# A two-layer hybrid decoder trunk on one core: the second layer's instructions placed by an event loop in place of the framework's scheduler

## Chip, core and metric

The kernel runs on one core of one Trainium2 chip, as one program. The metric is the device time in microseconds (us) from the program's start to its end; a kernel's time is the median of its runs. The engines are named as in the profile: PE (TensorE, matmul), PEld (its weight loads), DVE (VectorE), ACT (ScalarE), POOL (GpSimd) and SP (SyncE, which here issues nearly all DMAs). Each engine works off a queue of its own in the order in which the instructions stand there, and waits at an instruction until what it needs is done.

## What is computed

Two residual layers over 2048 tokens of width 1024 (float32). Layer 1 mixes by gated linear attention, layer 2 by dilated window attention in three groups of six heads; both add attention into 256 memory tokens, a SiLU gate and an output projection. The change lies in layer 2 and at the seam to it.

```python
DIL_GROUPS = ((128, 1), (512, 4), (2048, 16))   # window, dilation
DIL_HEADS, DIL_HEAD_DIM = 6, 128

def dilated_group(q, k, v, window, dilation):
    # tokens are sorted by phase (position mod dilation) and cut into blocks of 128;
    # each block sees itself and the block before it
    s = jnp.einsum('bphjqd,bphjkd->bphjqk', qb, kw) * (Dh ** -0.5)
    s = jnp.where(mask, s, -jnp.inf)
    m = jnp.max(s, axis=-1, keepdims=True)
    p = jnp.exp(s - m)
    den = jnp.sum(p, axis=-1, keepdims=True)
    o = jnp.einsum('bphjqk,bphjkd->bphjqd', p / den, vw)
    return o, (m + jnp.log(den))[..., 0]

def dilated_mixer(h, w_in):
    for g, (window, dil) in enumerate(DIL_GROUPS):
        qkv = (h @ w_in[:, base:base + 3 * 768]).reshape(B, T, 3, 6, 128)
        q, k = partial_rope(qkv[:, :, 0], pos), partial_rope(qkv[:, :, 1], pos)
        o, lse = dilated_group(q, k, qkv[:, :, 2], window, dil)
    wts = jax.nn.softmax(jnp.stack(lses, axis=0), axis=0)     # over the groups
    o = jnp.einsum('gbth,gbthd->bthd', wts, jnp.stack(outs, axis=0))
    q_mem, gate = jnp.split(h @ w_in[:, 3 * 3 * 768:], [256], axis=-1)
    return o, q_mem, gate

def reference(x, mem, ...):
    for i in range(2):
        h = rmsnorm(x, norm_w[i])
        mix, q_mem, gate = (gla_mixer if i == 0 else dilated_mixer)(h, ...)
        mem_o = memory_attention(q_mem, mem_n, w_memkv[i])
        x = x + (jnp.concatenate([mix, mem_o], -1) * jax.nn.silu(gate)) @ w_out[i]
    return rmsnorm(x, final_norm_w)
```

## The kernel before

**What sets the order.** The kernel is written against a tile framework. Pools hand out buffers, the framework adds the waits, and a scheduler inside it places each engine's instructions by a timeline of its own; the order in which the code emits them is a starting point. Nothing in layer 1 or 2 is fixed by hand before the change.

**Layer 1** ends with a stage that takes the 16 token blocks in pairs: `a2_q`, `a2_gate`, `a2_branch`, `a2_out`, `a2_norm`, and `a2_pair`, which forms seven sums and differences of the normalised rows (the left operands of a Strassen-Winograd scheme: seven products of half-size blocks in place of eight). Each is split into a high and a low fp16 part, transposed by DMA and kept as a tile `h2s[half][0..6]`, some straight in SBUF and some through DRAM (`h2_d`).

**Weight sets.** Layer 2's input projection is cut into 28 sets of 256 columns: nine for values (`v`), eighteen for queries and keys (`qk`, one head each) and one for the memory queries (`m`); four more sets are the gate. `load_ws` (L847) loads a set in float32 (`stg`), for `qk` scales one half of it (L853), and makes the seven right operands `w`: ACT writes the high part (L859), DVE the low part (L860), POOL the differences between (L863 to L869).

**Products.** `sw_half` (L875) runs one set against one half of the rows: seven products, each of 48 matmuls of 128 columns (values) or 12 of 512 columns (queries, keys, gates). Each goes to a PSUM bank from `mm_bank` (L832), which takes turns among five banks (`ps_mm` twice over, `ps_x`, `ps_tr`). ACT copies three results out (`snap`, L896: p1, u2, u3), POOL adds p1 to two of these, DVE adds a bank to a copy (`addto`, L901, tile `cx`), and `fin` splits each finished block into high and low (`hl`, L965 on ACT, L966 on DVE) and stores it to DRAM. A rotary embedding follows for each half of a `qk` set (`xr`, `sw`, L1008 to L1023).

**Attention.** 18 heads of 8 steps make 144 steps. `att_load` brings q, k and v back from DRAM. `att_scores` (L1054) computes two blocks of scores into `ps_g`, DVE takes the masked row maximum (L1087, `mx`, result `pm`) and the bias `st` (L1091), ACT the exponential (L1097). `split_P` makes high and low parts `ph` (ACT L168, POOL L169) and transposes them by DMA to `pt` (L170). The value products (`pv`, L1112) then read `pt` into `ps_o`. After eight steps `att_stats` transposes the statistics `st` (L1142) and stores them. When three groups of a head pair are done, `combos` (L1184) mixes them; its loads (`fo`, `fb`) and its work on POOL and DVE are strewn in twice during the products and once at the gates.

**Interleaving.** The code emits products and attention by a fixed pattern: `advance(to)` emits products up to a count, each attention step follows its count (L1281 to L1302), values lag scores by a step and two products.

**Gates.** `gate_half` (L1225) computes a sigmoid (tile `e`): a clamp on POOL or, where the source is a PSUM bank, on DVE (L1233), three ACT functions (L1234 to L1236), a product with the mixed heads on POOL (L1237) and one with the gate input on DVE (L1238). Between the gate products stand 16 blocks of memory attention (`mem_stage`, L1330), whose weights `mp` pass through `split_P` as `mh`. The output projection (L1389 to L1437) takes 16 row blocks in turn.

## Time and profile before

| | |
|---|---|
| median of 3 runs | 2891.72 us (2888.61 to 2911.24) |
| profiled execution | 2893.61 us, span 2891.5 us |
| granted PE clock, mean | 0.950 |
| HBM traffic | 280.44 MB read, 136.76 MB written |
| hand-over of the layers | about 973 to 1009 us |
| products and attention of layer 2 | about 1009 to 2427 us |
| gates and memory attention | about 2427 to 2707 us |
| output projection | about 2707 us to the end |

The page's second part gives the span in 40 equal slices, with the busy share of each engine in tenths (9 is 90% or more), the clock granted to PE in tenths, and the share of the DMA engines:

```profile
PE   7999889899999399899998787999787898768799
PEclk9999989999999799999999999999999999878999
DMA  6234952456466735777666889675788776776533
```

A slice is 72.3 us. The fourteenth (a 3) is the hand-over between the layers. The 7s and 8s after it come in two groups, in which the mixes of the first and second head pairs run, and at the end in the gate stage.

### The profile page before, as it was taken

The page shows a single profiled execution, that of the slowest core. Times are in us where ns is not written, and L with a number is a line of the kernel's source. Part 1 is how long each engine was busy: PE and PEld are TensorE (multiplying, and loading weights), DVE is VectorE, ACT ScalarE, POOL GpSimd, SP SyncE. Part 2 cuts the span into 40 slices and gives each one's busy share as a digit, 9 for nine tenths or more (in the row PEclk, how much of TensorE's full clock was granted, in tenths as well). Part 3 has the DMA queues.
Part 4 walks back from the last instruction along what each step waited for, and adds up shares of the span by engine and source line. Part 5 has one row for each costly group of instructions (what it writes and reads, how often), then busy time and mean ns, then how long its engine had stood idle before and what let it go on. Part 6 is the DMA issues. An engine that isn't in the chain of part 4 may idle for free. (4 is left out here: it accounts for less than half of the span.)

```text
span 2891.5 us, 55208 instructions
## 1 busy us (share of the span) xinstructions
PE 2526.5 (87%) x21384; PEld 1897.8 (66%) x21384; DVE 1621.2 (56%) x3141; ACT 1326.7 (46%) x2969; POOL 967.1 (33%) x789
## 2 busy tenths in 40 slices
PE   7999889899999399899998787999787898768799
PEld 6888779788887374757574655766464765334587
DVE  6446544565556346565656566565557556654433
ACT  6356643553444244455444344444444445454422
POOL 0000000021112135444544556343455444776300
PEclk9999989999999799999999999999999999878999
DMA  6234952456466735777666889675788776776533
GB/s 204 82 131 161 293 168 86 125 134 154 107 149 155 210 115 152 187 170 174 157 167 175 206 212 194 163 184 146 201 203 203 179 165 167 185 185 170 193 132 123
DMA packets 807659, 481.81 MB, mean 167 GB/s; under 512 B 509234, under 2 KB 746468, under 8 KB 806244
## 3 DMA queue, kind: packets, MB, share of 16 engines
q1 hardware_dynamic: 807396, 478.28, 63.7%
q8 instruction: 168, 2.75, 0.4%
q14 instruction: 95, 0.78, 0.1%
HBM read 280.44 MB, written 136.76 MB: 144 GB/s over the span
## 5 line engine op out<-in xcount | busy, mean ns | idle before, releaser
L175 PE MATMUL ps_mm<-w,hT 128*128 128x256 f16 (+1 forms) x1408 | 390.8, 278 | 17.8 <-ACT v L529 6.2
L176 PE MATMUL ps_mm<-w,hT 128*128 128x256 f16 (+1 forms) x1408 | 390.0, 278 | 0.0
L177 PE MATMUL ps_mm<-w,hT 128*128 128x256 f16 (+1 forms) x1408 | 388.6, 278 | 0.4 <-DVE hT L421 0.4
L176 PEld LDWEIGHTS <-w 128*128 128x128 f16 x2032 | 210.2, 103 | 160.2 <-issue 46.7
L177 PEld LDWEIGHTS <-w 128*128 128x128 f16 x2032 | 209.7, 103 | 145.3 <-issue 14.5
L175 PEld LDWEIGHTS <-w 128*128 128x128 f16 x2032 | 210.4, 104 | 129.0 <-issue 12.3
L860 DVE SCALAR_TENSOR_TENSOR w<-stg,wsc,w 128x512 f16<-128x512 f32 x217 | 199.6, 920 | 160.6 <-ACT w L859 159.7
L169 POOL TENSOR_TENSOR stg<-mp,stg 128x512 f16<-128x512 f32 x16 | 18.9, 1180 | 724.4 <-ACT stg L168 724.4
L859 ACT ACTIVATE w<-stg,wsc 128x512 f16<-128x512 f32 x217 | 155.2, 716 | 201.7 <-DMA stg<-in_w_in_b 85.1
L1097 ACT ACTIVATE pm<-pm,st,qsc 128x256 f32<-128x256 f32 (+1 forms) x288 | 156.7, 545 | 180.0 <-DVE st L1091 179.2
L169 POOL TENSOR_TENSOR ph<-pm,ph 128x512 f16<-128x512 f32 (+2 forms) x144 | 149.6, 1040 | 210.4 <-ACT ph L168 122.6
L175 PE MATMUL ps_mm<-w,w 128*128 128x128 f16 (+1 forms) x744 | 186.4, 280 | 8.9 <-DVE cx L901 8.7
L966 DVE SCALAR_TENSOR_TENSOR hl<-cx,hl 128x512 f16<-128x512 f32 x162 | 140.1, 865 | 94.5 <-ACT hl L965 93.1
L176 PE MATMUL ps_mm<-w,w 128*128 128x128 f16 (+1 forms) x744 | 186.3, 280 | 0.0
L177 PE MATMUL ps_mm<-w,w 128*128 128x128 f16 (+1 forms) x744 | 186.0, 279 | 0.0
L965 ACT ACTIVATE hl<-cx 128x512 f16<-128x512 f32 x162 | 100.9, 623 | 184.9 <-DVE cx L901 158.7
L176 PEld LDWEIGHTS <-hT 128*128 128x128 f16 x1408 | 140.3, 100 | 39.6 <-issue 19.8
L175 PE MATMUL ps_o<-pt,v 128*128 128x128 f16 (+1 forms) x384 | 79.2, 235 | 86.9 <-DMA pt<-ph 86.8
L175 PEld LDWEIGHTS <-hT 128*128 128x128 f16 x1408 | 140.7, 100 | 21.2 <-issue 1.3
L177 PEld LDWEIGHTS <-hT 128*128 128x128 f16 x1408 | 140.5, 100 | 19.5 <-DVE hT L421 0.7
L918 POOL TENSOR_TENSOR u<-u,p 128x512 f32<-128x512 f32 x64 | 88.2, 1379 | 120.9 <-ACT u L896 119.9
L175 PEld LDWEIGHTS <-h 128*128 128x128 f16 x800 | 89.2, 112 | 37.7 <-issue 35.9
(419 smaller groups left out, 8087.7 us busy)
## 6 DMA issues: line engine op xcount, KB each, us to landing
stg<-in_w_in_b SPq DMA_DIRECT2D x144, 256.0 KB
stg<-in_w_in_b SPq DMA_DIRECT2D x54, 512.0 KB
qkd<-hl SPq DMA_DIRECT2D x144, 192.0 KB
rope<-in_rope SPq DMA_DIRECT2D x36, 512.0 KB
vud<-hl SPq DMA_DIRECT2D x72, 256.0 KB
q<-qkd SPq DMA_DIRECT2D x72, 256.0 KB
od<-osb SPq DMA_DIRECT2D x72, 256.0 KB
fb<-fd SPq DMA_DIRECT2D x72, 256.0 KB
```

The source lines that it names most:

```text
L169: G.tensor_tensor(out=lo, in0=src, in1=hi, op=ALU.subtract)
L175: PE.matmul(o, sh, mh, start=first, stop=False, skip_group_check=free)
L176: PE.matmul(o, sh, ml, start=False, stop=False, skip_group_check=free)
L177: PE.matmul(o, sl, mh, start=False, stop=last, skip_group_check=free)
L859: A.activation(out=t[:, 0], in_=src, func=AF.Copy, scale=s1)
L860: V.scalar_tensor_tensor(out=t[:, 1], in0=src, scalar=s1, in1=t[:, 0], op0=ALU.mult, op1=ALU.subtract)
L918: G.tensor_tensor(out=u3, in0=u3, in1=p1, op=ALU.add)
L965: A.activation(out=hi, in_=src, func=AF.Copy, scale=SQ)
L966: V.scalar_tensor_tensor(out=lo, in0=src, scalar=SQ, in1=hi, op0=ALU.mult, op1=ALU.subtract)
L1097: A.activation(out=p_, in_=p_, func=AF.Exp, scale=sc, bias=st[:, sj[jj]:sj[jj] + 1], accum_out=st[:, 16 + sj[jj]:17 + sj[jj]])
```

## The change

From the end of layer 1 on, `tc.manual_schedule()` keeps every engine's instructions in the order in which the code emits them. That order is made by a loop of events, `Flow`. Every strand of work (a weight set, a product's copy, a softmax, a mix) is a Python generator that asks for an engine ("P", "A", "V", "G", "S" for SP, "D" for the DMA transfer) with a duration written in the code, waits a time ("t"), waits for an event ("w") or takes a buffer ("g"). `Flow` hands each engine to the waiting strand of the lowest priority number, and the instruction is emitted when its turn comes in the plan.

```diff
+    def kick(self, e):
+        if self.busy.get(e, 0) or not self.wait[e]:
+            return
+        _, _, th, d = heapq.heappop(self.wait[e])
+        self.busy[e] = 1
+        self.at(self.now + d, self.freed, e, th, self.step(th))
...
-    def mm_bank():
-        turn[0] += 1
-        return bank((ps_mm, ps_x, ps_mm, ps_tr)[turn[0] % 4])
...
+        yield from prod(0)
+        yield "g", s_bank["a"]
+        yield "P", 2.6
+        ta = bank(ps_mm)
+        pr(ta, 0, True)
+        yield from done(0)
+        fl.spawn(snap(ta, "p1", "p1", False), 0)
...
+        yield from prod(2)
+        yield "w", eg["p1"]
+        yield "P", 2.6
+        pr(ta, 2, False)
```

A half's seven products follow each other strictly, over three banks: two of `ps_mm` (a, b) and one of `ps_x` (c). Before each product, `unit_jobs` emits what is ready by plan: statistics, then values, then scores.

```diff
+    def due(k):
+        un = k // 16
+        return 28 + LEAD + 42 * un + ((42 if un < 8 else 18) * (k % 16)) // 16
+
+    def unit_jobs():
+        while True:
+            if stat and stat[0].e_st.set:
+                yield from stats(stat.pop(0))
+            elif pend and pend[0].ready():
+                yield from values(pend.pop(0))
+            elif step[0] < 144 and nprod[0] >= due(step[0]) and len(pend) < 3 and s_sb.n and \
+                    heads[step[0] // 8].e_ld[step[0] % 8 // 2].set:
+                H, n = heads[step[0] // 8], step[0] % 8
+                step[0] += 1
+                yield from scores(H, n)
...
+        yield "A", 0.62
+        A.activation(out=ph[:, :width], in_=pm[:, :width], func=AF.Copy)
+        yield "G", 1.25
+        G.tensor_tensor(out=ph[:, width:2 * width], in0=pm[:, :width], in1=ph[:, :width], op=ALU.subtract)
+        yield "t", 0.1
+        fl.put(s_pm)
+        yield "g", s_pt
+        pt = pv.pt = tl(pk3, [P, 8, P], F16, "pt")
+        yield "S", 1.3
+        SY.dma_start_transpose(pt[:, :2 * width // P, :], ph[:, :2 * width])
+        yield "t", 2.4
+        fl.put(s_ph)
+        yield "t", 1.2
+        fl.fire(pv.ev)
...
+        fl.spawn(weights(wsets[0], raw0), 1)
+        fl.spawn(load_h2(), 0)
+        fl.spawn(rest_weights(), 2)
+        fl.spawn(mixes(), 3)
+        seq = [(0, 0), (1, 0), (0, 1), (1, 1)] + [(n, hf) for n in range(2, len(sets)) for hf in range(2)]
```

The last line is the start of the product stage: the first `v` set and the first `qk` set both run on half 0 of the rows, then both on half 1. The second set's operands then need buffers of their own; they take idle ones of the attention (`pm`, `ph`, `pt`).

Softmax and copies of products have priority 0, the first weight set 1, further weights 2, the mixes 3. Smaller parts: a raw weight set is loaded by one DMA for each column block in place of two; a half's rotary rows are stored by two DMAs of 64 partitions in place of four of 32; `cx` has four buffers in place of three and also holds what were `osb` and `sw`; `pt` has three buffers in place of two; the statistics go to `ps_tr`; memory attention takes its row maximum and exponential half by half; in layer 1 a staging buffer moves to another pool, so that the pool of weight operands no longer waits for it. At the gates the clamp goes to DVE or POOL by the load in the plan, the gate sets run in the order 0, 1, 3, 2, the memory blocks are paced by the count of products, and the third mix is a strand of its own:

```diff
-            (V if ps else G).tensor_scalar(out=e, in0=src, scalar1=neg, scalar2=87.0, op0=ALU.mult, op1=ALU.min)
+                if ps or fl.load("V") <= fl.load("G"):
+                    yield "V", 0.65
+                    V.tensor_scalar(out=e, in0=src, scalar1=neg, scalar2=87.0, op0=ALU.mult, op1=ALU.min)
+                else:
+                    yield "G", 1.35
+                    G.tensor_scalar(out=e, in0=src, scalar1=neg, scalar2=87.0, op0=ALU.mult, op1=ALU.min)
```

The orders of the two kernels show what moved. Their rows give the line, the operation, the tile written and the tiles read, with the program's numbers, and the shape. Lines after the change have numbers of their own.

The first place is ACT's queue at the seam of the layers. Before, with L778 the last piece of `a2_pair`, L853 the scaling of the second weight set and L859 the operands of the first:

```order
L778 ACTIVATE stg_11322<-x_11073 128x512
L853 ACTIVATE stg_11430<-stg_11430,wrat_5384 128x8x128
L859 ACTIVATE w_11405<-w_11185,wsc_5382 128x512
L859 ACTIVATE w_11410<-w_11185,wsc_5382 128x512
L859 ACTIVATE w_11414<-w_11185,wsc_5382 128x512
L859 ACTIVATE w_11417<-w_11185,wsc_5382 128x512
L859 ACTIVATE w_11421<-w_11185,wsc_5382 128x512
```

After, where L876 is that last piece, L986 the operands, L1064 a copy of a product, L977 the scaling of the second set, and the operand written to `pm` the second set's first:

```order
L876 ACTIVATE stg_11342<-x_11093 128x512
L986 ACTIVATE w_11426<-w_11205,wsc_5386 128x512
L1064 ACTIVATE p_1600_11485<-ps_mm_11435 128x512
L986 ACTIVATE w_11487<-w_11205,wsc_5386 128x512
L986 ACTIVATE w_11493<-w_11205,wsc_5386 128x512
L986 ACTIVATE w_11496<-w_11205,wsc_5386 128x512
L977 ACTIVATE stg_11430<-stg_11430,wrat_5388 128x8x128
L986 ACTIVATE pm_11550<-stg_11430,wsc_5386 128x512
L1064 ACTIVATE u_1607_11601<-ps_mm_11498 128x512
L986 ACTIVATE w_11603<-w_11205,wsc_5386 128x512
```

The second set's scaling has moved from ahead of all of the first set's operands to behind four of them, and three of the first set's stand behind it.

The second place is ACT's queue at the end of the attention. Before, with L1097 the exponential, L168 the split, and L896 the copies of gate products:

```order
L1097 ACTIVATE pm_29519,st_29015<-pm_29519,st_29015,qsc_5385 128x128 x2
L896 ACTIVATE u_3965_29780<-ps_mm_29767 128x512
L168 ACTIVATE ph_29531<-pm_29519 128x256
L1097 ACTIVATE pm_29547,st_29015<-pm_29547,st_29015,qsc_5385 128x128 x2
L168 ACTIVATE ph_29559<-pm_29547 128x256
L896 ACTIVATE u_3980_29876<-ps_mm_29767 128x512
L1097 ACTIVATE pm_29573,st_29015<-pm_29573,st_29015,qsc_5385 128x128 x2
```

After, with the exponential at L1423, the split at L1429 and the copies of products at L1064:

```order
L1423 ACTIVATE pm_29500,st_28292<-pm_29500,st_28292,qsc_5389 128x128 x2
L1423 ACTIVATE pm_29521,st_28292<-pm_29521,st_28292,qsc_5389 128x128
L1429 ACTIVATE ph_29534<-pm_29500 128x256
L1423 ACTIVATE pm_29521,st_28292<-pm_29521,st_28292,qsc_5389 128x128
L1429 ACTIVATE ph_29547<-pm_29521 128x256
L986 ACTIVATE w_29551<-stg_29350,wsc_5386 128x512
L1064 ACTIVATE p_3957_29652<-ps_mm_29634 128x512
```

The copies of gate products that stood among the last exponentials now follow behind all of them.

The third place is POOL's queue in the gate stage. Before, with L1233 the clamp, L169 the low part of the memory weights, L1237 the gate product and L1202 to L1207 the mix:

```order
L1207 TENSOR_TENSOR fb_30212<-fb_30212,fb_30167 128x512
L1233 TENSOR_SCALAR e_30730<-cx_30726,wneg_5386 128x512
L1233 TENSOR_SCALAR e_30810<-cx_30806,wneg_5386 128x512
L169 TENSOR_TENSOR mh_30548<-mp_30545,mh_30548 128x512
L169 TENSOR_TENSOR mh_30555<-mp_30552,mh_30555 128x512
L1237 TENSOR_TENSOR e_30608<-e_30608,oc_30606 128x512
```

After, with L1754 the clamp, L1842 the low part, L1764 the gate product, L994 a difference of weights, L1070 the add to a copy of a product and L1618 the mix:

```order
L1618 TENSOR_TENSOR fb_30673<-fb_30673,fb_30609 128x512
L1842 TENSOR_TENSOR mh_30758<-mp_30726,mh_30758 128x512
L1842 TENSOR_TENSOR mh_30779<-mp_30728,mh_30779 128x512
L1764 TENSOR_TENSOR e_30781<-e_30781,oc_30754 128x512
L994 TENSOR_TENSOR stg_30382<-stg_30382 128x4x128
L1070 TENSOR_TENSOR u_4186_30848<-u_4186_30848,p_4145_30645 128x512
L1842 TENSOR_TENSOR mh_30889<-mp_30838,mh_30889 128x512
```

The low parts no longer stand behind clamps; in all, 9 of the 24 clamps that POOL did remain there and 15 have gone to DVE.

More of the change, by code (lines that the diff above doesn't have):

```diff
@@ L251, in mem_sc @@
         ps = []
-        sb = [bank(ps_g) for hh in range(2)]
         for hh in range(2):
-            s = sb[hh]
+            s = bank(ps_g)
             for jj in range(2):
@@ new lines, in prod, with done @@
+        def prod(n):
+            yield from jobs()
+            yield "w", W.ev[n]
+            yield "w", h2ev[hf][OPS[n]]
+        def done(n):
+            yield "t", 0.0
+            nprod[0] += 1
+            if hf == 1:
+                fl.put(W.home[n][0])
+            if last is not None and OPS[n] not in (3, 4):
+                fl.put(last)
+        yield from prod(0)
+        yield "g", s_bank["a"]
+        yield "P", 2.6
+        ta = bank(ps_mm)
+        pr(ta, 0, True)
+        yield from done(0)
@@ L1078, in blk @@
             return t[:, e, :].rearrange("p (l r) -> p r l", r=4)[:, b_, :]
[L1080 removed]
+        yield "P", 0.6
+        s = bank(ps_g)
+        blks = []
+        at = 0
+        for j in js:
             w = 2 if j % nb > 0 else 1
[L1082 removed]
             o = s[:, at:at + w * P]
@@ L1255, in trunk, with stored @@
+    def stored(h, c, og, sg_):
+        yield from dma(acc_d[h][c], og, 256, 0.4)
+        fl.put(sg_)
+        fl.fire(e_acc[h][c])
     sets = [("v", 0, 0), ("qk", 0, 0)]
@@ L1417, in trunk @@
                 o0 = cs.start % 512
+                yield "g", s_ob2
+                yield "P", 5.5 * n / 512
+                turn[0] += 1
+                t = bank((ps_mm, ps_x, ps_mm, ps_o)[turn[0] % 4])
                 for k in range(KT):
```

1372 lines of the change are left out of this document (955 added, 417 removed).

## The prediction

> **What bounds the kernel now.** I read the page's engine totals first, then the span cut into stages, then TensorE's waits in each stage.
>
> ```profile
> PE 2526.5 (87%) x21384; PEld 1897.8 (66%) x21384; DVE 1621.2 (56%) x3141; ACT 1326.7 (46%) x2969; POOL 967.1 (33%) x789
> ```
> TensorE (PE) is busy for 87% of the span and no other engine for more than 66%: the kernel gains only where PE stands, or runs at a lower granted clock. The next view cuts the span into stages (columns: width, then busy time and instructions of PE, PEld, DVE, ACT and POOL, granted PE clock, DMA share, GB/s).
>
> ```profile
> 973.00:1009.00 36.00, 0.27 (x1) 0.20 (x2) 8.05 (x7) 6.53 (x11) 6.20 (x4) 0.55 0.92 272
> 1009.00:1100.00 91.00, 87.97 (x897) 61.70 (x897) 39.99 (x56) 35.16 (x57) 36.20 (x30) 0.97 0.39 127
> 1100.00:1190.00 90.00, 80.43 (x493) 43.57 (x491) 58.43 (x114) 45.21 (x96) 45.78 (x40) 0.96 0.66 172
> 1190.00:1490.00 300.00, 283.95 (x2793) 200.17 (x2791) 182.00 (x375) 147.87 (x330) 138.70 (x121) 0.98 0.72 169
> 1490.00:1800.00 310.00, 261.25 (x2256) 171.64 (x2253) 189.07 (x355) 134.50 (x290) 157.37 (x131) 0.95 0.80 194
> 1800.00:2000.00 200.00, 191.03 (x1939) 136.76 (x1939) 120.91 (x255) 97.66 (x222) 87.03 (x78) 0.99 0.67 164
> 2000.00:2300.00 300.00, 245.50 (x2217) 166.67 (x2216) 178.94 (x327) 124.99 (x269) 154.60 (x124) 0.93 0.81 194
> 2300.00:2427.00 127.00, 120.90 (x1289) 89.13 (x1287) 73.84 (x171) 59.67 (x151) 54.29 (x50) 1.00 0.71 170
> 2427.00:2707.00 280.00, 195.51 (x1075) 101.85 (x1075) 158.84 (x223) 153.82 (x332) 202.18 (x134) 0.82 0.72 183
> 2707.00:2892.00 185.00, 177.83 (x901) 149.51 (x899) 64.58 (x83) 46.05 (x114) 1.29 (x1) 0.99 0.39 137
> ```
> All before 973 us is layer 1. From 973 to 1009 PE stands for a hand-over. The product stage (1009 to 2427) is 1418 us wide; its PE column sums to 1271.0, so PE stands for 147.0, and width times (1 - clock) sums to 50.8 more. That loss of 197.8 sits mostly in the two stretches where the mixes run (1490 to 1800 and 2000 to 2300): 610 us wide, 103.3 idle and 36.5 of clock, 139.8 together, at a DMA share of 0.80. The gate stage (2427 to 2707) loses 84.5 and 50.4. The output projection has 177.8 busy of 185 at clock 0.99, so it holds little. What PE waits for, first in the product stage, then at the hand-over, then in the gate stage (columns: us in total, times, longest):
>
> ```profile
> PE ps_o L175 <- DMA pt<-ph: 86.1, 41, 5.7
> PE ps_g L175 <- DVE mx L1087: 25.0, 21, 4.6
> PE ps_g L1142 <- ACT pm L1097: 15.2, 4, 7.1
> PE ps_x L175 <- ACT p L896: 6.0, 4, 2.0
> PE ps_x L175 <- DVE cx L901: 2.7, 1, 2.7
> ...
> PE ps_x L175 <- ACT w L859: 36.4, 1, 36.4
> ...
> PE ps_o L286 <- DMA mp<-mh: 33.5, 12, 4.9
> PE ps_x L1420 <- ACT w L1385: 11.7, 1, 11.7
> PE ps_mm L175 <- DVE cx L901: 6.1, 2, 3.9
> PE ps_x L175 <- DVE e L1238: 5.5, 1, 5.5
> ```
> The largest wait is that of the value products (into ps_o) for the transposed softmax weights pt: 86.1 of the 147.0. Waits for product banks (the ps_x and ps_mm rows of the product stage) are small.
>
> **Layer 1.** The weight pool no longer waits for a staging buffer, and sixteen more small DVE operations appear. No row shows PE waiting for either: 0, with 5 either way.
>
> **Hand-over.** Three rows of ACT:
>
> ```profile
> 989.66 0.63 ACT L778 ACTIVATE stg<-x 128x512 f16<-128x512 f32 x1 [1.04 <-POOL x L799]
> 1000.73 1.15 ACT L853 ACTIVATE stg<-stg,wrat 128x1024 f32<-128x1024 f32 x1 [10.43 <-DMA stg<-in_w_in_b]
> 1007.95 0.72 ACT L859 ACTIVATE w<-w,wsc 128x512 f16<-128x512 f32 x1 [6.07 <-DMA tq<-stg]
> ```
> ACT does its last layer-1 piece until 990.3, then stands in its queue for the second set's raw weights until 1000.7, and begins the first set's operand only at 1007.95. After the change that operand follows the last layer-1 piece directly, 17.7 us earlier: this is the upper end, -17. But only four operands stand ahead of the second set's scaling, which again waits for a raw load, now queued on SP behind the last h2 stores and loads. The first set's other operands stand behind it. If the load lands about where it did, PE gets an early start and loses half of it again. I take -8; ends -17 and 0. Beginning two sets on half 0 gives four halves' worth of products before half 1's seven operands are needed; from 1009 to 1100 PE is busy for 88 of 91, so it has nothing further to win there.
>
> **Product stage: pt.** One wait followed back, from the last score matmul to the first value matmul:
>
> ```profile
> 1320.12 0.38 PE L177 MATMUL ps_g<-k,q 128*128 128x256 f16 x2
> 1323.46 0.41 DVE L1087 CUSTOM_DVE_ANT_0 pm<-ps_g,mw 128x256 f32<-128x256 f32 x1
> 1324.14 0.22 DVE L1091 TENSOR_SCALAR st<-mx,qsc 128x2 f32<-128x2 f32 x1
> 1326.26 0.93 POOL L169 TENSOR_TENSOR ph<-pm,ph 128x384 f16<-128x384 f32 x1 [2.05 <-DVE cx L901]
> 1328.35 1.52 SPq L170 DMA_TRANSPOSE pt<-ph  x1
> 1332.94 0.27 PE L175 MATMUL ps_o<-pt,v 128*128 128x128 f16 x1 [4.78 <-DMA pt<-ph]
> ```
> From 1320.5 to 1332.94 the chain takes 12.4 us, and PE stood for 4.78 of it. Of the 12.4, 3.0 went by until DVE took the scores, 1.2 on SP (1327.19 to 1328.35), 4.6 from issue to use. The change cannot shorten the 4.6; it can shorten the 4.2 of queueing, because the loop gives the softmax chain the first rank on DVE, ACT and SP. It does not give it more room on PE: counted over the 144 steps of the two orders, 4.0 products lie between a step's scores and its values before and 3.9 after. A product is about 2.7 us (87.97 us from 1009 to 1100 hold 672 matmuls of fourteen products of 48 and 225 of products of 12, so 32.75 products). Four are some 10.7 us; against a chain of 12.4 - 4.2 = 8.2 that leaves 2.5 us. The mean wait is 2.1 (86.1 over 41). So the typical one goes, and those with a slow transfer stay: I take 0.7 of 86.1, -60; ends 0 and -86.
>
> **mx and the statistics.** The scores are issued only when their bank is free by plan (the 25.0), and the transpose of the statistics (the 15.2) is put off until its exponentials are done by plan and moves to another bank: three quarters of 40.2, -30; ends 0 and -40.
>
> **Fewer banks.** Products use three banks in a fixed order in place of five. The nearest rows are ps_x behind ACT's copy and DVE's add (8.7 together, ends 0 and that again): I take +8. Queued behind such a wait are the next scores and values, and so the next head's chain.
>
> **Clock.** In the trace a short stand lowers the granted clock:
>
> ```profile
> 1443.79 0.22 PE L175 MATMUL ps_o<-pt,v 128*128 128x128 f16 x1 [2.08 <-DMA pt<-ph]
> ...
> 1443.00:1450.00 7.00, 6.21 (x27) 2.84 (x27) 3.68 (x9) 1.23 (x3) 3.26 (x4) 0.76 0.71 179
> ```
> After a gap of 2.08 us the next 7 us were granted 0.76. So I let the clock loss shrink with idle time: (60 + 30 - 8) / 147.0 of 50.8, -28; ends 0 and -50.8. [...]
>
> The product stage comes to -60 - 30 + 8 - 28 = -110.
>
> **Tail of attention.** Before, gate products stand among the last scores and values; after, the last steps follow each other with no products between, and the gate products come behind them. Four waits of up to 5.7 (the longest pt wait) are uncovered at most, +23; none at the least. I take +15.
>
> **Gate stage.** Rows of POOL and DVE there:
>
> ```profile
> L1233 POOL TENSOR_SCALAR e<-cx,wneg 128x512 f32<-128x512 f32 x24 | 49.3, 2062 | 8.5 <-DMA brd<-e 5.4 <-DVE cx L901 3.1
> L1238 DVE SCALAR_TENSOR_TENSOR e<-cx,winv,e 128x512 f32<-128x512 f32 x23 | 26.0, 1135 | 9.8 <-POOL e L1237 9.8
> L860 DVE SCALAR_TENSOR_TENSOR w<-stg,wsc,w 128x512 f16<-128x512 f32 x17 | 20.8, 1222 | 10.2 <-ACT w L859 10.2
> L1238 DVE SCALAR_TENSOR_TENSOR e<-ps_mm,winv,e 128x512 f32<-128x512 f32 x4 | 3.0, 746 | 3.1 <-POOL e L1237 3.1
> L1233 DVE TENSOR_SCALAR e<-ps_mm,wneg 128x512 f32<-128x512 f32 x4 | 3.0, 740 | 0.1
> ```
> Fifteen of the 24 POOL clamps go to DVE: 15 x 2.06 = 31 off POOL's 202.2, and 15 x 0.74 = 11 onto DVE's 158.8. Both then have about 170 of work in a stage where PE has 195.5. So I take three quarters of the mp waits (33.5), -25; most of the two waits behind cx and e (6.1 + 5.5), -10; and half of the 50.4 of clock, -25. Together -60. Ends: 0, and -109, where POOL's 171 alone would set the stage.
>
> **The rest at nothing.** The 11.7 us wait for the output weights stays, since they are still loaded only beside the last gate half; the output projection is dense. Some 120 fewer DMA issues on SP (raw weights in one piece, rope rows in two) are hidden: no PE row above waits for either. If SP lay on the path they would show in the chain to pt, and are counted there.
>
> **Sum.** -8 - 110 + 15 - 60 = -163. The profiled execution took 2893.6 (span 2891.5), which gives 2730.6. The median of the runs is 2891.7, 0.07% lower, so 2729.
>
> **Rivals.**
> - *Nearly all goes* (0.12). For it: every wait above is one that an order can avoid. -17 at the hand-over, the whole 197.8 of the product stage, -60 at the gates: 2893.6 - 275 = 2619, about 2617. Against it: the 4.6 us of the transfer and 0.80 of DMA share stay.
> - *Transfers hold the mix stretches* (0.20). Where the mixes run the DMA share is 0.80 and 0.81 at 194 GB/s, against 0.67 to 0.72 beside them, and the change moves the same bytes. If the 139.8 us stay there, half of the 58.0 lost in the rest of the product stage goes (-29), half of the gates' 60 (-30), 8 at the hand-over, and the tail gives back 5: 2893.6 - 62 = 2832, about 2830.
> - *POOL and DVE hold each other up* (0.08). An operation of DVE with two SBUF sources takes 1135 ns and the same from PSUM 746, while POOL works. If POOL's 202.2 and DVE's two-source rows (26.0 + 20.8) had to follow each other, they fill 249 of the 280; after the change 249 - 31 + 11 = 229, so the gate stage wins only 20 in place of 60: 2770.6, about 2769. [...]
> - *Waits change place* (0.08). Four products after the scores are as many as before; if the chain stays at 12.4 us the waits stay and nothing moves: within 1%, 2892.
> - *Slower: the fixed order with three banks* (0.09). Before, a late copy by ACT delays one bank of five, and the scheduler has other products ready. After, the third product of a half must wait for the copy of the first, and whatever ACT has ahead of it stands on the path. There are 64 halves. Without the 8 for banks the gain is 171, or 2.7 us for each half, one product's time: there it decides. At two products (5.3) a half, 64 x 5.3 = 339: 2893.6 - 171 + 339 = 3062, about 3060. Against it: ps_x behind ACT costs 6.0 in all now.
>
> **How the numbers follow.** The forecast of 2729 has 0.43. About 1% (29 us) is what the measurement can tell from no change: faster by over 1% (below 2863) are the forecast, the first three rivals: 0.43 + 0.12 + 0.20 + 0.08 = 0.83; same 0.08; slower 0.09. The range reaches over the transfers' case above (2830 and some 20) and down to a little under the first rival's 2617: 2605 to 2850. Outside it lie the slower case (0.09), the waits that change place (0.08) and a third of the first rival (0.04), 0.21 together. The forecast's own range is 2680 to 2800.
>
> **What would show it.** Hand-over: PE's wait ahead of the first product falls from 36.4 to about 28. Product stage: the pt waits fall to about 26, mx and statistics to 10, the clock in the two mix stretches rises over 0.95. Gates: the mp waits are under 10 and POOL is near 171. Tail: PE stands some 15 us between the last product and the first gate product. I am wrong if the pt waits stay at 86, if PE's waits for ACT's copies (p, u) rise over 20, or if the mix stretches keep losing 140.

## Result: 2.5% faster, less than half of what was forecast

| | before | after |
|---|---|---|
| median, us | 2899.93 (2888.61 to 2911.24, 4 runs) | 2827.76 (2823.69 to 2830.73, 4 runs) |
| profiled execution, us | 2893.61, span 2891.5 | 2825.64, span 2823.8 |
| ratio to before | | 0.975, 95% interval 0.970 to 0.980 |

The time fell by 68 us between the two profiled executions, where the forecast had 163. The changed kernel's engine totals, from the page's first part:

```profile
PE 2507.7 (89%) x21384; PEld 1895.5 (67%) x21384; DVE 1626.9 (58%) x3172; ACT 1341.5 (48%) x2969; POOL 942.1 (33%) x774
```

The work of the two kernels has to be lined up before stages are compared. Before the change the first gate products run among the last attention steps; after it they come behind them. The cuts below are therefore at PE's work: first product, last product of the 28 sets, last value product, last gate product, first matmul of the output projection. Columns are as in the prediction: width, then busy time of PE, PEld, DVE, ACT and POOL, granted PE clock, DMA share, GB/s. Before (the second row holds the first gate products together with the last attention steps):

```profile
1009.00:2402.00 1393.00, 1247.17 (x11720) 856.32 (x11720) 831.16 (x1614) 634.86 (x1381) 664.53 (x561) 0.96 0.73 177
2402.00:2427.00 25.00, 23.86 (x152) 13.32 (x150) 12.03 (x35) 10.21 (x31) 9.44 (x10) 1.00 0.59 160
2427.00:2690.00 263.00, 190.23 (x1062) 97.85 (x1061) 150.11 (x215) 142.83 (x317) 189.04 (x127) 0.84 0.74 184
2690.00:2702.00 12.00, 0.33 (x2) 0.00 (x0) 5.80 (x6) 7.33 (x11) 9.79 (x5) 0.65 0.67 213
```

After (the second row is the bare end of the attention, the third the gates, the fourth the wait for the output projection):

```profile
997.00:2351.00 1354.00, 1240.32 (x11718) 856.07 (x11718) 818.29 (x1618) 651.15 (x1390) 662.49 (x557) 0.96 0.78 183
2351.00:2374.00 23.00, 7.49 (x64) 5.79 (x62) 7.83 (x24) 7.24 (x20) 8.05 (x8) 0.63 0.79 190
2374.00:2614.00 240.00, 195.02 (x1151) 100.81 (x1150) 164.01 (x235) 140.96 (x319) 169.69 (x118) 0.92 0.84 205
2614.00:2635.00 21.00, 0.97 (x4) 0.47 (x3) 12.76 (x13) 14.24 (x18) 12.68 (x8) 0.63 0.67 198
```

Layer 1 ended 6 us earlier (966 in place of 972); the kernels below, whose layer 1 is that of the changed kernel, end it between 959 and 972, so these 6 us can't be told from chance. The hand-over took 30 us in place of 37. From the first product to the last the stage lost 39 us (1393 to 1354), of the 110 forecast: PE's idle time in it fell by 32 (145.8 to 113.7) and its busy time by 7. From the last product to the last gate product it is 288 before and 263 after, 25 less; in the sum below this stands as +23 for the bare end and -48 for the gates (288 against 240). The wait for the output projection grew from 12 to 21. The sum, -6 - 7 - 39 + 23 - 48 + 9, is the 68.

PE's waits between the first and the last product tell why the largest stage gave so little. After (columns: us in total, times, longest):

```profile
PE ps_o L275 <- DMA pt<-ph: 90.4, 32, 8.6
PE ps_x L275 <- DMA w<-h2d: 6.4, 1, 6.4
PE ps_o L275 <- DVE hl L1178: 4.4, 1, 4.4
PE ps_mm L275 <- ACT w L986: 4.2, 1, 4.2
PE ps_g L275 <- DMA k<-qkd: 3.7, 5, 1.3
PE ps_tr L1503 <- ACT pm L1423: 3.5, 8, 1.8
```

The scores' wait for their bank (25.0 before) is gone, that of the statistics fell from 15.2 to 3.5, and none for the product banks is left. The wait of the values for pt is as large as before, 90.4 against 86.1: in fewer and longer pieces.

### The profile page after: what moved, and what is told of

It reads as the page before. It is cut to its first block, busy times and chain, and to the rows that moved or that the text cites. A ratio compares the mean times of both kernels' runs of the same rounds, so it can differ in the third digit from the quotient of the medians.

```text
span 2823.8 us, 54912 instructions
## 1 busy us (share of the span) xinstructions
PE 2507.7 (89%) x21384; PEld 1895.5 (67%) x21384; DVE 1626.9 (58%) x3172; ACT 1341.5 (48%) x2969; POOL 942.1 (33%) x774
## 5 line engine op out<-in xcount | busy, mean ns | idle before, releaser
L277 PEld LDWEIGHTS <-w 128*128 128x128 f16 x1976 | 204.1, 103 | 145.8 <-issue 10.8
L276 PEld LDWEIGHTS <-w 128*128 128x128 f16 x1976 | 204.9, 104 | 132.0 <-issue 19.6
L275 PEld LDWEIGHTS <-w 128*128 128x128 f16 x1976 | 204.9, 104 | 128.2 <-issue 8.8
L988 DVE SCALAR_TENSOR_TENSOR w<-stg,wsc,w 128x512 f16<-128x512 f32 x210 | 205.5, 979 | 86.1 <-ACT w L986 83.4
L275 PE MATMUL ps_mm<-w,w 128*128 128x128 f16 (+1 forms) x976 | 240.1, 277 | 1.8 <-ACT u L1064 1.8
L276 PE MATMUL ps_mm<-w,w 128*128 128x128 f16 (+1 forms) x976 | 239.8, 276 | 0.0
L277 PE MATMUL ps_mm<-w,w 128*128 128x128 f16 (+1 forms) x976 | 239.7, 276 | 0.0
L1070 POOL TENSOR_TENSOR u<-u,p 128x512 f32<-128x512 f32 x128 | 178.0, 1390 | 171.8 <-ACT u L1064 164.1
L994 POOL TENSOR_TENSOR stg<-stg 128x512 f32<-128x512 f32 x124 | 174.6, 1409 | 139.3 <-DVE w L988 131.5
L1423 ACT ACTIVATE pm<-pm,st,qsc 128x256 f32<-128x256 f32 (+1 forms) x288 | 157.1, 546 | 106.5 <-DVE st L1417 105.4
L1431 POOL TENSOR_TENSOR ph<-pm,ph 128x512 f16<-128x512 f32 (+2 forms) x144 | 157.6, 1095 | 139.4 <-ACT ph L1429 103.4
L1178 DVE SCALAR_TENSOR_TENSOR hl<-cx,hl 128x512 f16<-128x512 f32 x162 | 127.3, 786 | 88.2 <-ACT hl L1176 87.5
L275 PE MATMUL ps_o<-pt,v 128*128 128x128 f16 (+1 forms) x384 | 80.4, 238 | 108.9 <-DMA pt<-ph 104.3
L986 ACT ACTIVATE w<-stg,wsc 128x512 f16<-128x512 f32 x210 | 148.9, 712 | 24.5 <-POOL stg L994 16.9
```

The lines of the kernel that those rows point to most:

```text
L275: PE.matmul(o, sh, mh, start=first, stop=False, skip_group_check=free)
L276: PE.matmul(o, sh, ml, start=False, stop=False, skip_group_check=free)
L277: PE.matmul(o, sl, mh, start=False, stop=last, skip_group_check=free)
L986: A.activation(out=t[:, 0], in_=src, func=AF.Copy, scale=s1)
L988: V.scalar_tensor_tensor(out=t[:, 1], in0=src, scalar=s1, in1=t[:, 0], op0=ALU.mult, op1=ALU.subtract)
L994: G.tensor_tensor(out=o_, in0=i0, in1=i1, op=ALU.subtract)
```

## Experiments

The question was why the waits for pt stayed, and whether the 71 us that the product stage owed lay there. Three theories: PE reaches the values too early, since the plan is short of the real chain (room); pt is issued late, behind other work in SP's queue (SP); the transfers of the mixes make it land late (transfers).

### Room: where the values stand

The three kernels differ from the changed one in one number, the planned time from the issue of pt to its landing: 6.2 us, 8.8 us and 1.0 us in place of 3.6.

```diff
         yield "S", 1.3
         SY.dma_start_transpose(pt[:, :2 * width // P, :], ph[:, :2 * width])
         yield "t", 2.4
         fl.put(s_ph)
-        yield "t", 1.2
+        yield "t", 3.8
         fl.fire(pv.ev)
```

> The plan lets a step's values be issued 2.6 us later after the transposing DMA (planned landing 6.2 us after the issue in place of 3.6), so that on PE five products stand between a step's scores and its values in place of four. Theory room (the chain from scores to pt is simply longer than the plan says: on the 38 waiting steps SP takes pt 3.3 us after POOL and it lands 5.8 us after the issue): each wait shrinks by one product, 2.7 us, the pt waits fall from 104 to about 35, the long gaps from 17 to about 7, and the time from 2828 to about 2740. Rival transfers (the DMA engines set the pace in the last half of the product stage, share 0.83 and 0.86): the waits come back elsewhere, as late loads of k and v, and the time stays between 2800 and 2828. Rival chain: two steps less lead for the next head, 2828 or more.

For the second, the same line has 6.4:

> As the first experiment with another 2.6 us: values are planned 8.8 us after the issue of pt, so that six products stand between a step's scores and its values on PE (four in the changed kernel, five in the first experiment, 2788 us). Theory room: the pt waits left in the middle of the stage (about 30 of the 49) go too, and the time falls by another 20 to 35, to about 2760. Rival transfers: the DMA share is at 0.87 to 0.89 in the second half of the stage already, so the time stays within 12 us of 2788 and the waits go to PE's other inputs (k, copies p and u).

For the third, the values are released first and the buffer after:

```diff
-        yield "t", 2.4
-        fl.put(s_ph)
-        yield "t", 1.2
+        yield "t", 1.0
         fl.fire(pv.ev)
+        yield "t", 1.4
+        fl.put(s_ph)
```

> The opposite of the first experiment: the plan lets values follow 1.0 us after the issue of pt in place of 3.6, so that of the 144 steps 94 have three products between scores and values on PE and 39 have four (mean 3.3; 3.9 in the changed kernel). Theory room: the pt waits rise by about the 1.8 us that are missing on every second or third step, from 104 to 200 or more, and the time from 2828 to between 2880 and 2930: with four, five and six products it makes one curve. Rival: the waits are set by late transfers and by SP's queue whatever the place of the values, the pt waits stay under 140 and the time within 25 us of 2828.

PE's wait for pt over the whole run, in the kernel with less room, the first and the second with more (the changed kernel's is 104.3 in 37 waits, the longest 8.6):

```profile
PE ps_o L275 <- DMA pt<-ph: 199.1, 77, 11.8
```
```profile
PE ps_o L275 <- DMA pt<-ph: 48.6, 17, 7.9
```
```profile
PE ps_o L275 <- DMA pt<-ph: 20.4, 5, 9.2
```

And the stage from the first product to the last, in the same order:

```profile
989.00:2470.00 1481.00, 1275.89 (x11735) 870.11 (x11735) 789.83 (x1616) 650.62 (x1390) 661.73 (x558) 0.94 0.71 168
```
```profile
991.00:2309.00 1318.00, 1225.79 (x11703) 845.13 (x11703) 825.11 (x1612) 645.34 (x1386) 668.04 (x556) 0.98 0.80 189
```
```profile
997.00:2296.00 1299.00, 1222.20 (x11705) 838.70 (x11705) 820.70 (x1605) 642.16 (x1379) 676.61 (x556) 0.98 0.82 190
```

| products between scores and values, mean | pt waits, us | stage, us | median, us | ratio to before (interval) |
|---|---|---|---|---|
| 3.2 (less room) | 199 | 1481 | 2943.1 | 1.016 (1.010 to 1.021) |
| 3.9 (the change) | 104 | 1354 | 2827.8 | 0.975 (0.970 to 0.980) |
| 4.8 (room) | 49 | 1318 | 2788.5 | 0.963 (0.959 to 0.967) |
| 5.6 (room, twice) | 20 | 1299 | 2776.9 | 0.959 (0.955 to 0.962) |

One number of the plan spans 166 us, and decides whether there is a gain at all: at 1.0 us the kernel is slower than before the change. The waits themselves follow the theory closely (expected 35 at the first, measured 49; 200 or more at the third, measured 199). The time does not go all the way with them: the first was expected at 2740 and stands at 2789, the second at 2760 and stands at 2777, the third at 2880 to 2930 and stands at 2943. As pt stops holding PE, smaller waits show: ACT's copies p rise to 17.6 us and the statistics to 14.3 in the first kernel, from nothing and 3.5. Room is a cause, but not all of what was missing.

### SP's queue

One stand of 8.60 us in the changed kernel, as the trace has it, POOL first, then SP, then PE:

```profile
1703.24 1.41 POOL L1431 TENSOR_TENSOR ph<-pm,ph 128x384 f16<-128x384 f32 x1
...
1704.93 3.57 SPq L947 DMA_DIRECT2D rope<-in_rope  x1
1708.60 0.52 SPq L1589 DMA_DIRECT2D fo<-od  x1
1709.17 0.61 SPq L1594 DMA_DIRECT2D fb<-fd  x1
1709.88 0.38 SPq L947 DMA_DIRECT2D od<-cx  x1
1710.35 0.57 SPq L1247 DMA_DIRECT2D qkd<-hl  x1
1711.03 2.71 SPq L1437 DMA_TRANSPOSE pt<-ph  x1
...
1719.58 0.27 PE L275 MATMUL ps_o<-pt,v 128*128 128x128 f16 x1 [8.60 <-DMA pt<-ph]
```

The low part is done at 1704.65, and pt is issued at 1711.03, behind five other issues; it serves PE 8.55 us later. The plan had 4.9 us for this last stretch, from the start of the issue to the landing. Three runs tried to shorten the stretch before it.

Transposes issued by ACT:

```diff
-        yield "S", 1.3
-        SY.dma_start_transpose(pt[:, :2 * width // P, :], ph[:, :2 * width])
+        yield "A", 1.5
+        A.dma_start_transpose(pt[:, :2 * width // P, :], ph[:, :2 * width])
```

> The 144 transposing DMAs are issued by ACT in place of SP. Theory SP order (pt stands on SP behind stores that wait for late data): the time from POOL's ph to the issue of pt falls from 1.5 us on average to under 0.5, the pt waits from 104 to about 50, and the time to about 2780; ACT pays 144 x 1.5 = 216 us of issue time, which its 48% load hides. Rival landing (the wait is the transfer itself): the waits stay over 85, the time within 15 us of 2828. Rival ACT: it now stands for POOL before each issue, its copies of products come late, PE waits for p and u, and the time is over 2850.

It took 2875.8 us (0.993, 0.990 to 0.997), and the pt waits rose to 131.2. The time is that of the rival with ACT, but its sign is missing: in the product stage PE waits for the copies p and u by 2.7 and 0.5 us. The issue did come sooner, as the theory asked: on the mean of the 144 steps 0.5 us after POOL's ph in place of 1.5. But POOL's ph came 0.6 us later after the scores, and the time from issue to landing (the last of the 16 completions that the trace has of each transfer) rose from 4.6 to about 6.4 us.

Other issues moved from SP to POOL (head, statistics and mix stores, mix loads; one of several like edits):

```diff
-            yield from dma(o_d[h][g][:, j4 * 512:(j4 + 1) * 512], osb, 256)
+            yield from gdma(o_d[h][g][:, j4 * 512:(j4 + 1) * 512], osb, 256)
...
+    def gdma(dst, src, kb):
+        yield "G", 0.6
+        G.dma_start(dst, src)
```

> The stores of the heads (od), of the statistics (std) and of the mixed heads (accd) and the loads of the first two mixes (fo, fb) are issued by POOL in place of SP, some 250 of SP's 1000 issues between the first product and the last, with the same transfers. Theory SP queue (pt stands on SP behind issues and behind stores that wait for late data; 3.3 us from POOL's ph to the issue of pt on the steps that PE waits for): that time falls under 2 us, the pt waits from 104 to about 60, and the stage from 1355 to about 1320. Rival landing (5.8 us from issue to use): the waits stay over 85. Rival POOL: its own issues cost it more than SP's did and wait for DVE and the DMA, ph and the sums u come late, and the time is over 2840.

Stores of values, queries and keys later in the plan (the same line in both places where they are issued):

```diff
             fl.put(rel)
+            yield "t", 2.0
             d = vu_d[un][ni]
```

> The stores of values, queries and keys (vud, qkd) take their place on SP 2.0 us later in the plan, when what they store is done by the trace too. Theory SP queue, its waiting part (stores that stand on SP for DVE's hl hold up pt behind them: 123 us of such waits in 79 times): those waits fall to under 50, pt is issued sooner, pt waits fall from 104 to about 75 and the time by 15 to 25. Rival: the three hl buffers are held longer, ACT stands for them, and the time stays within 8 us of 2828 or rises.

PE's wait for pt in the kernel with fewer issues on SP, then in that with the later stores:

```profile
PE ps_o L275 <- DMA pt<-ph: 98.3, 37, 6.9
```
```profile
PE ps_o L275 <- DMA pt<-ph: 90.4, 36, 7.4
```

They took 2811.1 us (0.970, 0.967 to 0.974) and 2814.5 us (0.971, 0.967 to 0.974); both intervals overlap that of the changed kernel. In the first, the time from POOL's ph to the issue of pt did fall, on the steps that PE waits for from 3.3 to 1.8 us (each of the 144 steps followed in the trace from its ph to its first value matmul). But the time from issue to use rose there from 5.8 to 6.8, and the waits stayed. The second did not do what it was for: SP's stores still wait for hl by 87.7 us (expected under 50), and the mean time from ph to the issue stayed at 1.5. So SP's queue delays pt, as the stand above shows, but none of the three runs shortened the chain: from the last score matmul to the landing it took 11.6 us on the mean in the changed kernel, and about 13.1, 11.8 and 11.8 in these three. Where pt was issued sooner after ph, a later ph and a slower landing took the gain back. The theory is not borne out; as something else moved in each run, it is not cleanly refuted either.

### The mixes

The first two mixes left out; then only their loads kept; then only their work. The last two have exactly the changed kernel's order on PE. Of each edit one piece is shown.

```diff
     def mixes():
+        return
+        yield
         for hp in range(2):
```

> The mixes of the first two head pairs are left out (the gates read the third pair's mixed heads for all three), with their 48 + 48 loads of 256 KB, 16 stores, their issues on SP and their work on POOL and DVE. Theory transfers (the loads of the mixes keep the DMA engines full, so that pt lands late): the pt waits fall from 104 to about 50 and the time to about 2750. Theory room alone: pt waits fall by no more than 20 and the time by no more than 30, since SP's queue and the four products stay. If the time falls by more than 100, the mixes' transfers hold more than the pt waits.

```diff
-                G.tensor_tensor(out=fb, in0=fb, in1=acc, op=ALU.add)
+                if hp == 2:
+                    G.tensor_tensor(out=fb, in0=fb, in1=acc, op=ALU.add)
```

> The mixes of the first two head pairs keep their loads, stores and issues, and leave out their 80 operations on POOL and 32 on DVE (the mixed heads are then not mixed); the plan and so PE's order are those of the changed kernel. Theory transfers: the loads alone hold what the mixes cost, the stage from the first product to the last stays at 1335 us or more (1355 with the whole mixes, 1281 without any), and the pt waits stay over 80. Rival work: POOL and DVE, busy with the mix, bring ph and hl late; without that the stage falls to about 1290 and the pt waits to about 50.

(The operations left out are 48 on POOL and 32 on DVE, 80 in all.)

```diff
+                if hp < 2 and k > 1:
+                    yield "S", 0.6
+                    yield "g", sf
+                    yield "S", 0.43
+                    got[k] = got["og"], got["fb", k % 2]
+                    fl.spawn(landed(k), 2)
+                    continue
```

> The other half of the pair: each of the first two mixes loads its first two pieces and then works on these again and again (subtracting in place of multiplying, so that the values stay finite), 88 loads of 256 KB fewer, with the same plan and the same order on PE; the mixed heads are not computed. Theory transfers: the stage from the first product to the last falls from 1355 to about 1295, pt lands sooner and the pt waits fall to about 50. Rival work: the stage stays at 1335 or more. If each of the two runs takes about half of the 74 us, both count and neither is the cause alone.

The stage from the first product to the last, without the mixes, with their loads only, with their work only:

```profile
995.00:2276.00 1281.00, 1221.69 (x11729) 843.91 (x11729) 755.10 (x1569) 652.80 (x1393) 584.85 (x513) 0.98 0.74 173
```
```profile
991.00:2329.00 1338.00, 1234.61 (x11729) 852.30 (x11729) 760.23 (x1589) 650.86 (x1390) 583.55 (x513) 0.96 0.79 186
```
```profile
1001.00:2324.00 1323.00, 1229.96 (x11716) 851.42 (x11715) 816.90 (x1618) 650.41 (x1389) 673.80 (x557) 0.96 0.71 171
```

From 1354 the stage falls by 73 without the mixes, by 16 without their work and by 31 without their loads. The medians are 2773.7 (0.957, 0.953 to 0.962), 2801.4 (0.967, 0.962 to 0.971) and 2786.9 (0.963, 0.959 to 0.966); the first contains 72 us in which the gates wait for the third mix, so only its stage is compared. The loads weigh more than the work, and neither is the cause alone. The pt waits tell the same: 43.4 without the mixes, 89.9 with the loads alone, 84.3 with the work alone. With the loads gone and the DMA share down from 0.78 to 0.71, pt waits fell by only 20 of 104; the theory that transfers alone make pt late falls. Part of the 73, some 26 us, belongs to neither half: what is left is the order itself, which is free of the mixes only in the first of the three, and their 16 stores and small tables; these were not tested apart.

Then room and mixes together:

> The second room kernel without the first two mixes (the gates read the third pair's mixed heads). It tells whether the two causes add. If the mixes cost time only by making pt late, then with the room the stage from the first product to the last, 1299 us, falls by less than 15. If they hold the stage in another way (transfers of k, v and weights, turns on POOL and DVE), it falls by 30 or more, and the rest of the gain that was forecast lies there.

```profile
993.00:2236.00 1243.00, 1205.83 (x11696) 833.25 (x11696) 739.69 (x1553) 643.53 (x1379) 584.69 (x511) 0.99 0.76 178
```

The stage is 56 us below the 1299 of the second room kernel (median 2750.9; 0.948, 0.945 to 0.951; the wait at the gates is in it again). The two causes nearly add: room is worth 55 us of the changed kernel's stage (1354 to 1299), and the mixes another 56 with the room given (73 without it). What is left, PE busy for 1206 of 1243 at clock 0.99, is all but dense.

### The start on half the rows

```diff
-        seq = [(0, 0), (1, 0), (0, 1), (1, 1)] + [...]
+        seq = [(0, 0), (0, 1), (1, 0), (1, 1)] + [...]
```

> Of the change, the start on half the rows is undone: the first value set runs on half 0 and then on half 1, the first query set behind it; all else is as in the changed kernel. Theory: the seven operands of half 1 (1 MB each through DRAM) land before the first value set's half 0 is through only if the second set's half 0 fills the time; without it PE stands some 10 us at the eighth product, and the first quarter of the product stage grows from 337 to about 347. Rival: the loads land in time, the two orders are worth the same, and the time stays within 8 us of 2828.

The first quarter of the products (by their matmuls) took 348 us in place of 337, as expected, with PE's wait for half 1's operands grown from 6.4 us in all to 18.2:

```profile
PE ps_x L275 <- DMA w<-h2d: 9.3, 1, 9.3
PE ps_mm L275 <- DMA w<-h2d: 8.9, 2, 7.7
```

The hand-over itself is the same 30 us, so this start is not what shortened it. The whole stage took 1370 us in place of 1354. The time, 2834.0 us (0.978, 0.975 to 0.980), is within the 8 us of the rival and can't be told from that of the change.

### A better version

The second room kernel, with the end of the attention drawn together:

```diff
-        return 28 + LEAD + 42 * un + ((42 if un < 8 else 18) * (k % 16)) // 16
+        return 28 + LEAD + 42 * un + ((42 if un < 8 else 10) * (k % 16)) // 16
...
-        yield "t", 1.2
+        yield "t", 1.2 if un * 2 + i == 17 else 6.4
...
-        fl.fire(H.e_st)
+        fl.spawn(later(H.e_st, 3.0), 2)
```

> The second room kernel (six products, 2777 us), with the end of the attention drawn together: the last head's scores may come as soon as they are loaded, its values at the old plan of 3.6 us, and the transposes of the statistics 3 us later. Theory: the bare stretch behind the last product, 33 us there and 22 in the changed kernel, falls to about 20, and PE's waits for ACT at the statistics (26 us) go: 2750 to 2765. Rival: the last head's chain is as long as it is, whatever the order, and the time stays within 6 us of 2777.

It took 2753.2 us (2749.0 to 2761.1; ratio 0.950, 0.947 to 0.953), the fastest of the kernels that leave nothing out. The bare end fell from 33 to 22 us, PE's waits for ACT at the statistics from 25.9 to 1.0, and the last quarter of the products took 280 us in place of 285.

## Why the prediction was wrong

**The step that failed** is the one on pt: "against a chain of 12.4 - 4.2 = 8.2 that leaves 2.5 us. The mean wait is 2.1 ... So the typical one goes, and those with a slow transfer stay: I take 0.7 of 86.1, -60". It came out as +4 (86.1 to 90.4 up to the last product). The term that was mis-sized is the chain. The forecast took it from one step, 12.4 us, and let it shrink to 8.2. Followed over all 144 steps in the two traces, from the last score matmul to the landing of pt, it shrank from 12.9 to 11.6 us on the mean. To POOL's ph it fell from 7.9 to 5.5: here the first rank did its work. From ph to the issue on SP it rose from 1.1 to 1.5, and from issue to landing from 3.9 to 4.6. The values meanwhile came sooner, 12.7 us after the scores in place of 13.9 (their own wait for pt taken off). So the mean slack grew from 1.0 to 1.2 us, where the forecast had 2.5. Two things more kept the waits where they were.

First, the prediction compared means. It saw that the products between scores and values were as many as before (4.0 and 3.9) and gave every step the same slack. Before, that number was spread, and late values went with a late chain: over the steps up to the last product, pt was issued 6.3 us after the scores where three products lay between (22 steps), 8.8 with four (85 steps) and 11.5 with five (28 steps). After, 117 of 138 steps have four, whatever their chain. An even four products meets an uneven chain, and the longest wait is 8.6 in place of 5.7. The room experiments show that the place of the values sets these waits; that the old order fitted it step by step is read from the counts and was not tested.

Second, "the change cannot shorten the 4.6" from issue to use was taken as a constant. On the steps where PE waits it averaged 4.7 before and 5.8 after, at a DMA share of 0.78 in place of 0.73. Part of this is which steps wait: before, those that were issued late (13.0 us after the scores, against 9.0 over all steps, with 4.5 from issue to landing against 3.9), after, rather those with a slow transfer (8.6 after the scores against 7.0, with 5.7 to the landing against 4.6). Over all steps the median from issue to landing is 3.8 before and 4.2 after, but the slowest tenth begins at 5.1 and at 6.8 us. The code had 4.9 from the start of the issue: enough for the usual step, too early for the slow ones.

**The clock** (-28 forecast, granted 0.96 in the stage before and after) failed with it and by itself. It was let shrink with idle time; by the prediction's own measure, width times (1 - clock), the loss of the stage rose from 50 to 59 us. The traces show that it goes with the number of long gaps. Their record of the granted clock holds 1.0 and 0.5 alone; of the low stretches that begin in the stage, 12 last 3.4 us and 8 last 6.8 us before the change, and 5 last 3.4, 11 last 6.8 and 2 last 10.2 us after it. Three windows of 3.4 us before, around the 2.08 us gap that the prediction quoted, and after, a low stretch of 10.2 us that begins 4 us into the 8.60 us gap:

```profile
1441.00:1444.40 3.40, 1.32 (x12) 0.69 (x10) 1.09 (x3) 2.00 (x7) 2.13 (x3) 1.00 1.03 207
1444.40:1447.80 3.40, 3.40 (x10) 1.21 (x9) 1.85 (x4) 0.00 (x0) 1.26 (x1) 0.50 0.71 153
1447.80:1451.20 3.40, 3.40 (x19) 1.73 (x18) 2.94 (x5) 1.49 (x3) 1.73 (x1) 1.00 0.65 166
```
```profile
1715.10:1725.30 10.20, 5.72 (x21) 2.72 (x22) 0.95 (x2) 0.00 (x0) 2.33 (x2) 0.50 0.68 133
```

With gaps of 3 us or more a low step came in 14 of 15 cases before and 17 of 18 after; with gaps of 1.5 to 3 us in 6 of 20 and 2 of 6. There are fewer gaps after the change (24 of 1.5 us or more, against 35) and more long ones, so the time at half clock went from 96 to 113 us while the idle time fell. In the other runs' stages it goes the same way: 5 gaps of 3 us or more and 27 us at half clock with room twice and no mixes, 11 and 58 with room twice, 25 and 181 with less room. The gap of 2.08 us above is one of the 6 of 20: the prediction let it stand for all, where 14 such gaps had no low step. The low steps behind gaps of 1.5 to 3 us make 6 x 3.4 = 20 of the 96 us before the change, so removing short waits could bring back little.

**What held, and what was luck.** The hand-over: -8 forecast, -7 measured, by luck. The prediction let the first operand follow ACT's last piece of layer 1 directly; it comes 17.4 us behind that piece, as before 17.7. In both kernels it waits for the last pair's transposes, as the prediction's third row of ACT already said, so its new place in ACT's queue gained next to nothing (0.2 us). The gain lies ahead of it, where DVE's last normalisation waits for the store of x1, 9.16 us before and 2.76 after; why it lands sooner was not tested. Its row before, then after, and that of the operand after:

```profile
981.99 1.29 DVE L768 SCALAR_TENSOR_TENSOR x<-x,rs,nwb 128x1024 f32<-128x1024 f32 x1 [9.16 <-DMA x1d<-x]
```
```profile
969.98 1.28 DVE L866 SCALAR_TENSOR_TENSOR x<-x,rs,nwb 128x1024 f32<-128x1024 f32 x1 [2.76 <-DMA x1d<-x]
995.73 0.72 ACT L986 ACTIVATE w<-w,wsc 128x512 f16<-128x512 f32 x1 [17.45 <-DMA tq<-stg]
```

Scores and statistics: -30 forecast, -37 measured (25.0 and 15.2 to 0 and 3.5). Tail: +15 forecast, +23 in the trace, 7.5 of it busy, of which the waits for pt are 13.9. Gates: -60 forecast, -48 by the cut above. As the first gate products moved out of the tail, the two are better taken together: -45 forecast, -25 measured. POOL's busy time from the last product to the last gate product fell from 198 to 178, by 21 of the 31 worked out, the mp waits from 33.5 to 12.3. The rival in which POOL and DVE hold each other up gave tail and gates -5; what came lies halfway, and no run decides between them. Banks: +8 forecast and none seen with pt in the way; PE waits for ACT's copies by 17.6 only once room is given. The output projection was put at nothing and cost 9 more: ACT splits its first rows behind the exponentials of the last gate half.

```profile
PE ps_x L2097 <- ACT w L1984: 20.0, 1, 20.0
```

**The rivals.** The time, 2828, is that of "transfers hold the mix stretches" (2830), and the loss of those stretches did stay, which the prediction had also named as a sign of being wrong: from the first to the last operation of each mix, idle time and width times (1 - clock) come to 131 us before (1531 to 1805 and 1993 to 2264) and 130 after (1512 to 1945, and 1975 to the last product, 809 us in place of 545). Its reason holds only in part: of the 56 to 73 us that the mixes hold, the loads alone account for 31. "Waits change place" named the mechanism that did act on pt (as many products as before, so the waits stay) and gave it the whole kernel.

**What stays open.** Why the slow transfers of pt are slower after the change, when neither fewer issues on SP nor fewer transfers brought the time from issue to use back (6.8 and 5.8 us on the waiting steps), was not settled. Nor was a tail covered by gate products tried.

## What to carry to other kernels

A fixed plan needs slack for the spread of a chain, not for its mean; here one planned landing time, 1.0 to 8.8 us, moved the kernel by 166 us, and the trace of the planned kernel is where to read it. When a scheduler's order is replaced, compare the distribution of the distances that matter (scores to values, here), step by step, before crediting a wait as removed: equal means hid that the old order's distances went with the chain and the new one's are even. And count gaps by length: here 18 of 3 us or more and 6 of 1.5 to 3 us came with 113 us at half clock, 15 and 20 of them with 96.

## What was not expected of the hardware

Two issues on SP took far longer than is usual in the changed kernel's trace: the rope load above held the queue for 3.57 us where the median of its kind is 0.47, and pt's own issue 2.71 where the median is 1.31. ACT as issuer of the transposes cost some 50 us net (ratio 0.993 in place of 0.975), with their landing about 6.4 us after the issue in place of 4.6. With some 250 DMAs issued by POOL its busy time in the product stage was up by 138 us (662 to 800), with no loss of time (2811.1 us against 2827.8).
